# Softmax cross-entropy, one core: full loads alternate between the SyncE ring and the GpSimd ring

## The chip, the cores and the metric

The kernel runs on one core of a Trainium2 chip; the other cores are idle. The metric is the device time of one execution in microseconds, as a median of several runs on the same chip. The profile comes from one more look at such a run, taken by the hardware profiler; its span is some 1.8 us shorter than the time quoted. All runs of the two kernels compared here are in the fast state (granted clock 1.0).

## The reference

```python
def reference(logits, labels):            # logits 16 x 512 x 32000 float32, labels 16 x 512
    m = np.max(logits, axis=-1, keepdims=True)
    lse = np.log(np.sum(np.exp(logits - m), axis=-1)) + m.squeeze(-1)
    log_probs = logits - lse[..., None]
    return -log_probs[batch_index, seq_index, labels]
```

8192 rows of 32,000 logits are read once: 1048.6 MB. For each row the kernel needs the sum of exponentials (it leaves the maximum out) and one logit, the one that the label names.

## The kernel before

Each of the 128 partitions owns 64 rows (g = 0 to 63). A full load brings half a row per partition, 128 x 16,000 float32 (8.192 MB, printed by the profile as 8000.0 KB), into one of three buffers; ScalarE takes the exp in place and accumulates the sum. First and last rows are cut finer, so that the pipeline fills and drains quickly.

```python
W = 16000
data = ctx.enter_context(tc.tile_pool(name="data", bufs=3))
# ...
nc.gpsimd.iota(idx[:], pattern=[[V, G]], base=0, channel_multiplier=G * V)
nc.gpsimd.tensor_tensor(out=idx[:], in0=idx[:], in1=labs32, op=ALU.add)
for g in range(G):                         # 64 gathers of 128 single logits, all at the start
    nc.gpsimd.indirect_dma_start(
        out=lab_logit[:, g:g + 1], out_offset=None, in_=lg,
        in_offset=bass.IndirectOffsetOnAxis(ap=idx[:, g:g + 1], axis=1))
# ...
for j, (g, b, at, n) in enumerate(loads):  # 139 loads, 124 of them full
    if b not in buffers:
        buffers[b] = data.tile([P, W], FP32, tag="t", name="t")
    t = buffers[b]
    # ...
    nc.sync.dma_start(out=t[:, at:at + n], in_=lg_pg[:, g, c0:c0 + n])
    exp(g, t[:, at:at + n])                # ScalarE, in place, accum_out = the sum
    # ... log and subtraction for the rows near the end
```

A load waits for the exp that last used its buffer; the framework puts that wait on the issuing engine.

The softmax here doesn't subtract the row's maximum and nothing guards it: scores larger than these inputs give would overflow.

Of the kernel before, what the change touches and what calls it, by code (L numbers as in the profile page):

```python
# [1 line left out]

# [5 lines left out]

FP32 = mybir.dt.float32  # L10
I32 = mybir.dt.int32


EXP = mybir.ActivationFunctionType.Exp
LN = mybir.ActivationFunctionType.Ln
ALU = mybir.AluOpType
X = mybir.AxisListType.X


@with_exitstack  # L20
def kernel(
    ctx: ExitStack,
    tc: tile.TileContext,
    logits: bass.AP,
    labels: bass.AP,
    out: bass.AP,
):
    nc = tc.nc

    B, S, V = logits.shape  # L30
    P = 128
    G = B * S // P
    W = 16000


    lg = logits.rearrange("b s v -> (b s) v")
    lg_pg = lg.rearrange("(p g) v -> p g v", g=G)
    labels_pg = labels.rearrange("b s -> (b s)").rearrange("(p g) -> p g", g=G)
    out_pg = out.rearrange("b s -> (b s)").rearrange("(p g) -> p g", g=G)



    loads = []

    def plan(g, widths_by_buffer, order):

        n_buffers = 1 + max((l[1] for l in loads), default=-1)
        for b, i in order:
            ws = widths_by_buffer[b]
            loads.append((g, n_buffers + b, sum(ws[:i]), ws[i]))  # L50

    plan(0, [[4000, 4000, 8000], [16000]], [(0, 0), (0, 1), (0, 2), (1, 0)])
    for g in range(1, G - 2):
        plan(g, [[W], [W]], [(0, 0), (1, 0)])
    plan(G - 2, [[W], [10000, 6000]], [(0, 0), (1, 0), (1, 1)])
    plan(
        G - 1,
        [[7400, 5840, 2260], [4540, 3720, 2920, 1780, 1460, 1120], [960]],
        [(0, 0), (0, 1), (1, 0), (1, 1), (1, 2), (0, 2), (1, 3), (1, 4), (1, 5), (2, 0)],
    )  # L60
    assert sum(l[3] for l in loads) == G * V

    data = ctx.enter_context(tc.tile_pool(name="data", bufs=3))
    persist = ctx.enter_context(tc.tile_pool(name="persist", bufs=1))

    labs64 = persist.tile([P, G], mybir.dt.int64)
    labs32 = labs64[:].bitcast(I32).rearrange("p (g two) -> p g two", two=2)[:, :, 0]
    idx = persist.tile([P, G], I32)
    lab_logit = persist.tile([P, G], FP32)
    K = 10  # L70
    sums = persist.tile([P, G - 1, 5], FP32)
    sums_last = persist.tile([P, K], FP32)
    totals = persist.tile([P, G - 1], FP32)
    logsum = persist.tile([P, G - 1], FP32)
    res = persist.tile([P, G - 1], FP32)
    part = persist.tile([P, 1], FP32)
    logsum_last = persist.tile([P, 1], FP32)
    res_last = persist.tile([P, 1], FP32)

    ctx.enter_context(tc.manual_schedule())  # L80


    nc.scalar.dma_start(out=labs64[:], in_=labels_pg)
    nc.scalar.preload_act_table_set("natural_log_exp_and_others")  # L84
    nc.vector.memset(sums[:], 0.0)  # L85
    nc.gpsimd.iota(idx[:], pattern=[[V, G]], base=0, channel_multiplier=G * V)  # L86
    nc.gpsimd.tensor_tensor(out=idx[:], in0=idx[:], in1=labs32, op=ALU.add)  # L87
    for g in range(G):
        nc.gpsimd.indirect_dma_start(  # L89
            out=lab_logit[:, g:g + 1],  # L90
            out_offset=None,
            in_=lg,
            in_offset=bass.IndirectOffsetOnAxis(ap=idx[:, g:g + 1], axis=1),
        )


    buffers = {}
    col = {}
    n_exp = {}

    def exp(g, ap):
        k = n_exp.get(g, 0)
        n_exp[g] = k + 1
        s = sums[:, g, k:k + 1] if g < G - 1 else sums_last[:, k:k + 1]
        nc.scalar.activation(out=ap, in_=ap, func=EXP, accum_out=s)  # L105

    for j, (g, b, at, n) in enumerate(loads):
        if b not in buffers:
            buffers[b] = data.tile([P, W], FP32, tag="t", name="t")
        t = buffers[b]  # L110
        c0 = col.get(g, 0)
        col[g] = c0 + n
        nc.sync.dma_start(out=t[:, at:at + n], in_=lg_pg[:, g, c0:c0 + n])  # L113
        exp(g, t[:, at:at + n])

        left = len(loads) - 1 - j
        if left == 6:
            nc.vector.reduce_sum(out=totals[:], in_=sums[:], axis=X)  # L118
        if left == 4:
            nc.scalar.activation(out=logsum[:], in_=totals[:], func=LN)  # L120
            nc.vector.tensor_tensor(out=res[:], in0=logsum[:], in1=lab_logit[:, 0:G - 1], op=ALU.subtract)  # L121
        if left == 1:
            nc.vector.reduce_sum(out=part[:], in_=sums_last[:, 0:K - 1], axis=X)  # L123
    assert n_exp[G - 1] == K
    nc.sync.dma_start(out=out_pg[:, 0:G - 1], in_=res[:])

    nc.scalar.activation(out=logsum_last[:], in_=sums_last[:, K - 1:K], func=LN, bias=part[:])  # L127
    nc.vector.tensor_tensor(out=res_last[:], in0=logsum_last[:], in1=lab_logit[:, G - 1:G], op=ALU.subtract)  # L128
    nc.sync.dma_start(out=out_pg[:, G - 1:G], in_=res_last[:])


# [1 line left out]
_INS = ['logits', 'labels']  # L133
_OUTS = [((16, 512), 'float32')]


# [23 lines left out]
```

## Time and profile before

| | before |
|---|---|
| time, median of 3 runs | 2435.72 us |
| bytes read | 1048.67 MB, 431 GB/s over the span |
| DMA engines busy with logits | 99.8% |
| ScalarE busy | 72% |
| a full load, landing to landing | 18.90 us |
| an exp of one full load | 13.54 + 0.19 us |

The first fence is the profile's page of the kernel before. The rows with digits show the busy share, in tenths, of 40 equal slices of the span; the queue lines give packets, MB and the share of the 16 DMA engines' time; a group's line gives busy us, mean ns of one, then the engine's idle time before these instructions and what ended it.

```profile
span 2434.1 us, 807 instructions
...
DVE 1.3 (0%) x5; ACT 1748.9 (72%) x281; POOL 61.0 (3%) x70
...
DMA  9999999999999999999999999999999999999998
GB/s 421 422 421 433 425 438 431 427 438 438 433 426 436 438 434 426 435 438 434 426 435 436 435 430 431 436 435 430 431 436 438 431 427 436 438 433 426 438 433 377
...
q1 hardware_dynamic: 20304, 1048.62, 99.8%
q0 software_dynamic: 2048, 0.04, 0.1%
...
L105 ACT ACTIVATE t<-t 128x16000 f32<-128x16000 f32 (+5 forms) x139 | 1734.8, 12481 | 681.4 <-DMA t<-in_logits_dram 681.2
...
```

The DMA engines are full in every slice but the last and almost everything is on one queue, q1. ScalarE (ACT) idles 681 us, and what ends its idle time is a load. That makes the kernel DMA-bound. The wait on SyncE's queue looks large and is harmless:

```profile
...
SPq L113 <- ACT t L105: 2330.9, 125, 26.6
...
```

The columns are us in total, times and the longest wait. SyncE waits for free buffers because more than enough is queued already. In the timeline of the steady part (start us, us, what; in brackets the idle time before it) an exp starts every 18.9 us after 5.3 us of waiting:

```profile
...
386.87 13.54 ACT L105 ACTIVATE t<-t 128x16000 f32<-128x16000 f32 x1 [5.30 <-DMA t<-in_logits_dram]
...
405.78 13.54 ACT L105 ACTIVATE t<-t 128x16000 f32<-128x16000 f32 x1 [5.28 <-DMA t<-in_logits_dram]
...
```

And the windows view (us, then busy us and count of VectorE, ScalarE and GpSimd, granted clock, DMA share, GB/s; a share can print as 1.01, as neighbouring packet records overlap by some ns) separates the stretch with gathers from the one without:

```profile
...
61.50:301.00 239.50, 0.00 (x0) 172.21 (x25) 41.32 (x44) 1.00 1.01 427
301.00:2159.00 1858.00, 0.00 (x0) 1340.05 (x197) 0.00 (x0) 1.00 1.00 433
...
```

While gathers run, GB/s is 427 instead of 433. The trace also records every DMA packet. In the steady part one packet is one partition's row of a load, 64,000 bytes in 2361 to 2369 ns, and they stand end to end. Shorter rows at both ends of the kernel (4480 bytes in 173 ns, 32,000 in 1185 ns) put all sizes from 4480 bytes up within 2% of a line: 27.2 GB/s per engine, and 8 ns per packet. 16 engines at 27.2 GB/s are 435 GB/s, which is the ceiling that the Trainium skill derives ("DMA: Bandwidth & Descriptors", section "Where 436 GB/s comes from"). This trace agrees: the steady part is within 0.4% of it.

### The profile page before, as it was taken

What the parts mean: (1) busy time and instruction counts of PE and PEld (TensorE: products, weight loads), DVE (VectorE), ACT (ScalarE), POOL (GpSimd) and SP (SyncE); (2) the same over time, 40 slices, a digit from 0 to 9 for tenths busy, and PEclk for the clock granted to TensorE, in tenths of its full rate; (3) what the DMA queues carried; (4) which work ended last, traced back from release to release, by engine and by line L of the source; (5) the groups of instructions that cost most, each with busy time, mean ns of one, the idle gap of its engine ahead of it and who ended that gap; (6) DMA issues with size and microseconds to landing.
All of it is one profiled execution on the core that took longest, in us unless ns stands there. A gap on an engine that the chain in (4) does not pass through costs nothing.

```text
span 2434.1 us, 807 instructions
## 1 busy us (share of the span) xinstructions
DVE 1.3 (0%) x5; ACT 1748.9 (72%) x281; POOL 61.0 (3%) x70
## 2 busy tenths in 40 slices
DVE  0000000000000000000000000000000000000000
ACT  4777766777677776777677776777667776777769
POOL 3222000000000000000000000000000000000000
DMA  9999999999999999999999999999999999999998
GB/s 421 422 421 433 425 438 431 427 438 438 433 426 436 438 434 426 435 438 434 426 435 436 435 430 431 436 435 430 431 436 438 431 427 436 438 433 426 438 433 377
DMA packets 22502, 1048.77 MB, mean 431 GB/s; under 512 B 4576, under 2 KB 4704, under 8 KB 5216
## 3 DMA queue, kind: packets, MB, share of 16 engines
q1 hardware_dynamic: 20304, 1048.62, 99.8%
q0 software_dynamic: 2048, 0.04, 0.1%
q10 hardware_dynamic: 144, 0.07, 0.0%
q14 instruction: 6, 0.05, 0.0%
HBM read 1048.67 MB, written 0.03 MB: 431 GB/s over the span
## 4 chain that ended last, share of the span: by engine, by line
DMA 76%; ACT 24%; issue 0%; SPq 0%; ACTq 0%; DVE 0%
DMA t<-in_logits_dram 76%; ACT t L105 24%; SPq L113 0%; ACTq L105 0%; ACT logsum_last L127 0%; DVE res_last L128 0%; ACT logsum L120 0%
## 5 line engine op out<-in xcount | busy, mean ns | idle before, releaser
L105 ACT ACTIVATE t<-t 128x16000 f32<-128x16000 f32 (+5 forms) x139 | 1734.8, 12481 | 681.4 <-DMA t<-in_logits_dram 681.2
L89 POOL DMA_INDIRECT lab_logit<-in_logits_dram,idx x64 | 60.3, 942 | 178.3 <-DMA lab_logit<-in_logits_dram,idx 174.5
L105 ACT ACTIVATION_READ_ACCUMULATOR t<-t 128x1 f32 x139 | 25.9, 186 | 0.0
L84 ACT ACT_TABLE_LOAD x1 | 1.3, 1283 | 1.2 <-PEq L144 1.2
L118 DVE TENSOR_REDUCE totals<-sums 128x63 f32<-128x315 f32 x1 | 0.5, 480 | 2398.9 <-ACT t L105 2398.9
L87 POOL TENSOR_TENSOR idx<-idx,labs 128x64 int32<-128x64 int32 x1 | 0.3, 322 | 7.5 <-DMA labs<-in_labels_dram 7.5
L85 DVE MEMSET sums<- 128x315 f32 x1 | 0.3, 321 | 0.9 <-PEq L144 0.9
L127 ACT ACTIVATE logsum_last<-sums_last,part 128x1 f32<-128x1 f32 x1 | 0.3, 294 | 0.0
L121 DVE TENSOR_TENSOR res<-logsum,lab_logit 128x63 f32<-128x63 f32 x1 | 0.2, 225 | 25.3 <-ACT logsum L120 25.3
L120 ACT ACTIVATE logsum<-totals 128x63 f32<-128x63 f32 x1 | 0.2, 238 | 0.0
L86 POOL IOTA idx<- 128x64 int32 x1 | 0.2, 172 | 0.4 <-PEq L155 0.4
L123 DVE TENSOR_REDUCE part<-sums_last 128x1 f32<-128x9 f32 x1 | 0.2, 163 | 4.0 <-ACT t L105 4.0
L128 DVE TENSOR_TENSOR res_last<-logsum_last,lab_logit 128x1 f32<-128x1 f32 x1 | 0.2, 159 | 1.2 <-ACT logsum_last L127 1.2
L144 POOL MEMSET const-uint8-127<- 128x1 uint8 x1 | 0.1, 118 | 0.0
L144 POOL MEMSET const-bfloat16-1.0<- 128x1 bf16 x1 | 0.1, 113 | 0.0
L144 POOL MEMSET const-float32-0.0<- 128x1 f32 x1 | 0.1, 98 | 0.2 <-issue 0.2
L144 POOL MEMSET const-float32-1.0<- 128x1 f32 x1 | 0.1, 104 | 0.0
## 6 DMA issues: line engine op xcount, KB each, us to landing
t<-in_logits_dram SPq DMA_DIRECT2D x124, 8000.0 KB, 43.0
t<-in_logits_dram SPq DMA_DIRECT2D x1, 5000.0 KB, 35.9
t<-in_logits_dram SPq DMA_DIRECT2D x2, 2000.0 KB, 9.6
t<-in_logits_dram SPq DMA_DIRECT2D x1, 4000.0 KB, 21.4
t<-in_logits_dram SPq DMA_DIRECT2D x1, 3700.0 KB, 32.9
t<-in_logits_dram SPq DMA_DIRECT2D x1, 3000.0 KB, 42.6
t<-in_logits_dram SPq DMA_DIRECT2D x1, 2920.0 KB, 39.5
t<-in_logits_dram SPq DMA_DIRECT2D x1, 2270.0 KB, 26.4
```

Source lines behind the costliest of these rows:

```text
L84: nc.scalar.preload_act_table_set("natural_log_exp_and_others")
L85: nc.vector.memset(sums[:], 0.0)
L86: nc.gpsimd.iota(idx[:], pattern=[[V, G]], base=0, channel_multiplier=G * V)
L87: nc.gpsimd.tensor_tensor(out=idx[:], in0=idx[:], in1=labs32, op=ALU.add)
L89: nc.gpsimd.indirect_dma_start(out=lab_logit[:, g:g + 1], out_offset=None, in_=lg, in_offset=bass.IndirectOffsetOnAxis(ap=idx[:, g:g + 1], ...
L105: nc.scalar.activation(out=ap, in_=ap, func=EXP, accum_out=s)
L118: nc.vector.reduce_sum(out=totals[:], in_=sums[:], axis=X)
L120: nc.scalar.activation(out=logsum[:], in_=totals[:], func=LN)
L121: nc.vector.tensor_tensor(out=res[:], in0=logsum[:], in1=lab_logit[:, 0:G - 1], op=ALU.subtract)
L123: nc.vector.reduce_sum(out=part[:], in_=sums_last[:, 0:K - 1], axis=X)
L127: nc.scalar.activation(out=logsum_last[:], in_=sums_last[:, K - 1:K], func=LN, bias=part[:])
L144: nc = _bacc.Bacc("TRN2", target_bir_lowering=False, num_devices=1)
```

## The change

The intent is to use both DMA rings that the core has, SyncE's hardware ring and GpSimd's software ring, in turn for the full loads numbered 4 to 123, and to spread the 64 gathers: as GpSimd's queue is in order, gathers ahead of its loads would hold them up, so two stand behind each GpSimd load until all 64 are out. Loads are also written ahead of the exp that precedes them, so that GpSimd's program order is right; buffers, sizes and exps stay.

```diff
+    shared = range(4, 124)
+
+    def ring(j):
+        return nc.gpsimd if j in shared and j % 2 == 1 else nc.sync
 ...
-    for g in range(G):
+    def gather(g):
         nc.gpsimd.indirect_dma_start(
 ...
+    to_gather = list(range(G))
 ...
-    for j, (g, b, at, n) in enumerate(loads):
+    def load(j):
+        g, b, at, n = loads[j]
         if b not in buffers:
             buffers[b] = data.tile([P, W], FP32, tag="t", name="t")
-        t = buffers[b]
 ...
-        nc.sync.dma_start(out=t[:, at:at + n], in_=lg_pg[:, g, c0:c0 + n])
-        exp(g, t[:, at:at + n])
+        ring(j).dma_start(out=buffers[b][:, at:at + n], in_=lg_pg[:, g, c0:c0 + n])
+        if ring(j) is nc.gpsimd:
+            for _ in range(2):
+                if to_gather:
+                    gather(to_gather.pop(0))
+
+    loaded = 0
+    for j, (g, b, at, n) in enumerate(loads):
+        while loaded < len(loads) and loads[loaded][1] < b + 3:
+            load(loaded)
+            loaded += 1
+        exp(g, buffers[b][:, at:at + n])
```

More of the change, by code (lines that the diff above doesn't have):

```diff
@@ L123 @@
             nc.vector.reduce_sum(out=part[:], in_=sums_last[:, 0:K - 1], axis=X)
-    assert n_exp[G - 1] == K
+    assert n_exp[G - 1] == K and not to_gather
     nc.sync.dma_start(out=out_pg[:, 0:G - 1], in_=res[:])
```

## The prediction

> **What bounds the kernel now.** The 16 DMA engines. The page's DMA row is 9 in all slices but the last, queue 1 keeps them busy for 99.8% of the span, and 1048.67 MB come in at 431 GB/s. ScalarE is busy 72% and in the steady part waits 5.27 us for each load (timeline): loads land every 18.90 us (56.70 us per three in the chain of waits), an exp takes 13.54 + 0.19 us. SyncE waits only for buffers (2330.9 us in total, 125 times): with three buffers, work is always queued.
>
> In the trace's packet records the steady part (301 to 2159 us) has 64,000-byte packets, one row each, of 2361 to 2369 ns, back to back: 8 and a 9 ns semaphore packet are the 18.90 us. Shorter rows (4480 bytes: 173 ns; 32,000: 1185 ns) put a line through these of 27.2 GB/s per engine plus about 8 ns per packet. The Trainium skill ("DMA: Bandwidth & Descriptors", section "Where 436 GB/s comes from") gives a ceiling of 435.2 GB/s; this trace runs at 433 in the steady part. At most 0.4% is left there, whoever issues.
>
> Outside it: about 2 us of start, about 6 us of gathers (early on three loads take 57.9 instead of 56.7 us), and a short tail.
>
> **What the change does.** 60 of the 124 full loads move to GpSimd's ring; buffers, bytes, exps and tail stay. The gathers spread from 247 us to some 1200 us.
>
> - Bandwidth: both rings feed the same 16 engines. The skill (same page, "Issuing engines are not separate DMA queues") says they interleave there and only issue time is saved; no run yet shows it for large loads. Issue time is hidden already. Gain 0.
> - Switching rings: in the gather period a 64,000-byte packet after a gather's 9 ns semaphore packet still takes 2361 to 2369 ns, so a switch costs nothing visible. Cost 0.
> - Gathers: each adds 24 ns of own packets per engine and makes the next large packet about 65 ns longer; 64 of them are about 6 us in either kernel. Change 0.
> - Software packets: a gather's 8 elements went as one 32-byte packet, so software packets can hold several descriptors. If a whole load's share (8 rows) went as one, 7 x 8 ns are saved per load, 60 loads: -3.5 us (estimate). If rows were cut into 4 KB packets, 15 x 8 ns per row would be added: about +58 us, 2.4%. I hold rows kept whole for much likelier.
> - Order: two loads now share the engines, so landings become uneven (about 16.5 and 21.3 us, or in pairs), but with three buffers one load's data is always queued when another is finished. No idle engine. GpSimd's issue is hidden behind queued work.
>
> **Predicted time:** 2433 us, 8 in 10 between 2427 and 2446. Faster by over 2%: 0.02; within 2%: 0.93; slower by over 2%: 0.05.
>
> **What would show it.** Right: DMA row still 9, two queues at about 50% each, sum of two landing intervals 37.8 us, ScalarE still 72% busy. Wrong: software packets under 64,000 bytes, DMA slices below 9, or steady GB/s off 433.
>
> **What would make it wrong.** Software packets cut small; descriptor fetch for the software ring slowing large packets; one engine lagging so that landings come late; a tail that starts out of phase; or gathers costing more beside software loads.

## The result

| | before | after |
|---|---|---|
| time, median of 4 runs each | 2435.72 us | 2436.28 us (2436.11 to 2436.45) |
| ratio of the fast runs | | 1.0002, 95% interval 0.9985 to 1.002 |
| GB/s over the span | 431 | 431 |
| ScalarE busy | 1748.9 us | 1746.8 us |

A ratio is the mean time of one kernel's fast runs over that of the other's of the same rounds, so it is not quite the ratio of the medians quoted.

The profile's page of the kernel after, the same parts as above and the group of GpSimd's loads:

```profile
span 2434.7 us, 804 instructions
...
DVE 1.3 (0%) x5; ACT 1746.8 (72%) x281; POOL 95.2 (4%) x130
...
DMA  9999999999999999999999999999999999999998
GB/s 422 437 424 434 437 422 437 436 425 434 435 425 435 435 423 437 435 423 437 435 423 436 437 434 426 436 436 435 428 433 436 436 429 430 437 437 432 426 436 374
...
q1 hardware_dynamic: 11664, 557.09, 53.1%
q0 software_dynamic: 10688, 491.56, 46.8%
...
L111 ACT ACTIVATE t<-t 128x16000 f32<-128x16000 f32 (+5 forms) x139 | 1734.4, 12478 | 683.4 <-DMA t<-in_logits_dram 683.3
L119 POOL DMA_DIRECT2D t<-in_logits_dram x60 | 33.3, 555 | 2160.0 <-ACT t L111 2120.1
...
```

The traffic is now split 53 to 47 over two queues, q1 (SyncE) and q0 (GpSimd), and little else on the page has moved: the DMA row is full, ScalarE's busy and idle times are those of before within 0.3%, and GpSimd is busy 95 us instead of 61. q0's packets add up as 60 loads x 128 rows = 7680, 60 x 16 semaphore packets = 960, and 2048 of the gathers (as before): 10,688. So the software ring sends whole rows of 64,000 bytes too; it neither cuts nor joins them. GpSimd's 60 issues cost it 0.56 us each.

The windows of the kernel after:

```profile
...
61.50:301.00 239.50, 0.00 (x0) 174.36 (x27) 14.91 (x18) 1.00 1.00 432
301.00:2159.00 1858.00, 0.00 (x0) 1327.22 (x197) 74.81 (x99) 1.00 1.00 433
...
```

The gathers' loss has moved, from the first 300 us (where it was 427 GB/s, now 432) into the long stretch, where it is too thin to show in these lines (from 300 to 1300 us it is 432 GB/s after and 434 before). In the packet records of one DMA engine (records do not name the engine; packets are strung together by each one's start meeting the end of the one before) the two rings take turns row by row:

```
start us   ns    bytes  queue
1602.337  2361   64000  q0
1604.695  2364   64000  q1
1607.055  2366   64000  q0
1609.417  2369   64000  q1
1616.504     9       4  q0     semaphore packet at the end of a load
1616.510  2366   64000  q1
```

(Two packets left out after the fourth. The starts are in the trace's own time, 10.46 us ahead of the time from the span's start in which the views count.) A change of ring costs nothing that these records show. The turn-taking agrees with the Trainium skill, "DMA: Bandwidth & Descriptors", section "Queues, rings and completion order": each engine goes round its rings packet by packet.

What did change is the rhythm. Timeline of the kernel after, while gathers stand behind the GpSimd loads:

```profile
...
1004.63 13.54 ACT L111 ACTIVATE t<-t 128x16000 f32<-128x16000 f32 x1 [17.08 <-DMA t<-in_logits_dram]
...
1018.17 13.52 ACT L111 ACTIVATE t<-t 128x16000 f32<-128x16000 f32 x1
...
1035.51 13.54 ACT L111 ACTIVATE t<-t 128x16000 f32<-128x16000 f32 x1 [3.73 <-DMA t<-in_logits_dram]
...
1049.83 13.54 ACT L111 ACTIVATE t<-t 128x16000 f32<-128x16000 f32 x1 [0.69 <-DMA t<-in_logits_dram]
...
1080.55 13.54 ACT L111 ACTIVATE t<-t 128x16000 f32<-128x16000 f32 x1 [17.09 <-DMA t<-in_logits_dram]
```

Exps start 13.5, 17.3, 14.3 and 30.7 us apart, in a repeating pattern of four loads in some 76 us, so the mean is still 18.9 us. It goes on until about 1440 us, some 200 us after the last gather; from then on they are 18.9 us apart, but for a few. ScalarE once waits 17 us for a load and once finds the next one there already. The DMA engines never run out meanwhile: in the packet records from 300 to 2200 us there is no moment with fewer than half of the engines active.

### The profile page after: what moved, and what is told of

Its sections match the earlier page's. It is cut to its first block, busy times and chain, and to the rows that moved or that the text cites. A ratio compares the mean times of both kernels' runs of the same rounds, so it can differ in the third digit from the quotient of the medians.

```text
span 2434.7 us, 804 instructions
## 1 busy us (share of the span) xinstructions
DVE 1.3 (0%) x5; ACT 1746.8 (72%) x281; POOL 95.2 (4%) x130
## 4 chain that ended last, share of the span: by engine, by line
issue 49%; DMA 36%; ACT 13%; another core or an unknown queue 1%; POOL 1%; SPq 0%; POOLq 0%; ACTq 0%; DVE 0%
DMA t<-in_logits_dram 36%; ACT t L111 13%; POOL t L119 1%; SPq L119 0%; POOL lab_logit L94 0%; POOLq L119 0%; ACT logsum_last L144 0%; ACTq L111 0%; DVE res_last L145 0%; ACT logsum L137 0%; POOLq L172 0%
## 5 line engine op out<-in xcount | busy, mean ns | idle before, releaser
L119 POOL DMA_DIRECT2D t<-in_logits_dram x60 | 33.3, 555 | 2160.0 <-ACT t L111 2120.1
L111 ACT ACTIVATION_READ_ACCUMULATOR t<-t 128x1 f32 x139 | 25.9, 186 | 0.0
```

The source lines that it names most:

```text
L111: nc.scalar.activation(out=ap, in_=ap, func=EXP, accum_out=s)
L119: ring(j).dma_start(out=buffers[b][:, at:at + n], in_=lg_pg[:, g, c0:c0 + n])
```

## Experiments

The theory to test: the time is the packet time of 16 engines, which ring sends a load does not matter to them, the gathers cost the same in both kernels, and the order of landings is absorbed by the buffers. The rivals: two effects cancel (a gain of two rings against a loss at the gathers, or the other way about), or the software ring has a cost that the hardware ring covers.

### Without gathers, both kernels

```diff
-    for g in range(G):
-        nc.gpsimd.indirect_dma_start( ... )
+    nc.gpsimd.memset(lab_logit[:], 0.0)        # kernel before; wrong result on purpose
```
```diff
-    to_gather = list(range(G))
+    to_gather = []                             # kernel after; wrong result on purpose
+    nc.gpsimd.memset(lab_logit[:], 0.0)
```

> The kernel before without its 64 gathers (wrong result on purpose: lab_logit is 0). Theory (time is the 16 engines' packet time, gathers cost the same in either kernel): about 6 us less than before, 2429.5 us (2428.5 to 2431), because each gather costs an engine 24 ns of its own packets and some 65 ns in the packet behind it. Rival (the spread gathers hide a gain or a loss of the second ring): nothing different is expected of this run alone, it must be read with after_no_gather.

> The changed kernel without gathers (wrong result on purpose), so loads on two rings alone. Theory: within 1 us of before_no_gather, about 2430 us, with both at about 433.7 GB/s in the steady part. Rival A (two rings carry more and the spread gathers take it back): 3 us or more below before_no_gather. Rival B (two rings cost something and spread gathers cost less): 3 us or more above it.

Measured: 2430.77 us (2430.72 to 2431.03) and 2431.16 us (2431.13 to 2431.45), beside 2435.72 us of the kernel before on the same chip. Both results are wrong, as intended. The gathers are worth 4.95 us before (2435.72 - 2430.77) and 5.12 us after (2436.28 - 2431.16, medians). The two rings alone differ by 0.4 us. So there is no pair of effects that cancel: loads on two rings gain nothing and lose next to nothing, and spreading the gathers neither saves nor costs.

Page of the kernel after without gathers, queue lines:

```profile
span 2429.4 us, 732 instructions
...
q1 hardware_dynamic: 11664, 557.09, 53.1%
q0 software_dynamic: 8640, 491.52, 46.8%
...
```

8640 = 7680 rows + 960 semaphore packets, with 2429.4 us of span beside 2434.7. In this kernel exps start 18.9 us apart from the tenth full load on; the pattern of 13.5 to 30.7 us is gone. So that pattern comes with the gathers behind the loads, not with the two rings as such. Why the gathers lock the loads into it I have not tried to settle; it costs no time here.

### All gathers ahead of the GpSimd loads

```diff
-    to_gather = list(range(G))
+    to_gather = []
+    for g in range(G):
+        gather(g)
```

> The changed kernel with all 64 gathers ahead of GpSimd's first load, as the kernel before has them. Theory: the engines' packet work is unchanged, but GpSimd's queue is in order and its first load (the sixth load of all) is issued only after the last gather; the trace of before shows the last gather at 247 us under full traffic, less when the engines run dry. The engines then idle some 50 to 110 us: 2490 to 2550 us, and afterwards the same pace. Rival (where the gathers stand does not matter, as gathers are cheap): 2436 us.

Measured: 2485.0 us (2484.95 to 2485.2), ratio 1.0202, correct. The direction is the theory's, the size is just under the range I gave. Windows and timeline of this kernel:

```profile
...
60.00:140.00 80.00, 0.00 (x0) 13.63 (x2) 42.67 (x46) 1.00 0.38 153
...
```

```profile
...
129.41 0.94 POOL L94 DMA_INDIRECT lab_logit<-in_logits_dram,idx  x1 [0.30 <-issue]
130.35 1.16 POOL L121 DMA_DIRECT2D t<-in_logits_dram  x2
152.26 13.54 ACT L113 ACTIVATE t<-t 128x16000 f32<-128x16000 f32 x1 [77.09 <-DMA t<-in_logits_dram]
...
```

From 60 to 140 us the engines are 38% busy, which is 0.62 x 80 = 49.6 us idle, and the kernel is 49.3 us slower. GpSimd's first load goes out at 130.35 us, behind the last gather, and ScalarE has waited 77 us for it. My range was too high because I took the gathers' slow pace under traffic (4.8 us each) too far: once the engines ran dry they went out every 1.25 us. Putting the gathers behind the loads is therefore a necessary part of this change, not an ornament.

### All full loads on GpSimd

```diff
-        return nc.gpsimd if j in shared and j % 2 == 1 else nc.sync
+        return nc.gpsimd if j in shared else nc.sync
```

> All 120 full loads from the fifth on through GpSimd's software ring, two gathers behind each of the first 32. Theory: the ring does not matter, rows stay whole packets of 64,000 bytes and GpSimd's issue is hidden behind a queued load: 2436 us (2434 to 2440), evenly spaced landings of 18.9 us as in before. Rival B (software-ring loads are slower by some per cent, and in the changed kernel the hardware ring filled their gaps): 2445 us or more.

Measured: 2445.60 us (2445.46 to 2445.7), ratio 1.004, correct. My expectation missed: this is the rival's number. But the windows show no slow ring in the steady part:

```profile
...
75.00:100.00 25.00, 0.00 (x0) 25.00 (x5) 4.66 (x6) 1.00 0.73 302
...
1300.00:2300.00 1000.00, 0.00 (x0) 722.32 (x106) 27.44 (x52) 1.00 1.00 434
...
```

434 GB/s from 1300 to 2300 us, as before; the loss is at the ends. From 75 to 100 us the engines are 73% busy (some 7 us lost): load 4, issued by GpSimd at 9 us, takes turns with SyncE's loads 2 and 3, which were issued earlier and are needed earlier (one engine's packet records alternate between the two rings from 13.5 to 40.6 us), so that load 2 lands at 41 us instead of 23 and its buffer comes free that much later. At the other end SyncE's last loads overtake the GpSimd loads before them (the records alternate again, from 2304 to 2339 us), and the timeline shows ScalarE waiting 24 us and then working through what has piled up, without a pause:

```profile
...
2306.41 13.54 ACT L111 ACTIVATE t<-t 128x16000 f32<-128x16000 f32 x1 [7.63 <-DMA t<-in_logits_dram]
...
2344.21 13.54 ACT L111 ACTIVATE t<-t 128x16000 f32<-128x16000 f32 x1 [24.17 <-DMA t<-in_logits_dram]
...
2357.75 13.52 ACT L111 ACTIVATE t<-t 128x16000 f32<-128x16000 f32 x1
...
```

That reading, hand-over between rings instead of a slow software ring, is a new theory, and needed its own run.

### Every load on GpSimd, from the first

```diff
-        return nc.gpsimd if j in shared and j % 2 == 1 else nc.sync
+        return nc.gpsimd
 ...        # iota and add for the gathers' indices are moved behind the first five loads;
 ...        # two gathers still follow each load from the fifth on
```

> All 139 loads of logits on GpSimd's software ring, the index arithmetic moved behind the first four loads. after_all_gpsimd took 2445.6 us instead of 2436; its trace shows 434 GB/s from 1300 to 2300 us as before, but 394 GB/s in the first 100 us, where a GpSimd load overtakes an earlier SyncE load, and ScalarE idle for 24 us at 2320 us, where SyncE loads overtake the last GpSimd loads. Theory (the loss is the change of ring at both ends, not the software ring): with one ring throughout it is gone, 2436 us (2434.5 to 2439), landings 18.9 us apart. Rival (software loads are slow to start or need more queued work): 2443 us or more again.

Measured: 2436.94 us (2436.91 to 2437.19), beside 2435.94 us of the kernel before: ratio 1.0004. The 10 us are gone; how they divide between the two ends was not measured. One ring throughout, of either kind, is the same speed within 0.04%:

```profile
span 2435.4 us, 803 instructions
...
q0 software_dynamic: 22000, 1048.62, 99.8%
...
```

### Two hardware rings

```diff
-        return nc.gpsimd if j in shared and j % 2 == 1 else nc.sync
+        return nc.scalar if j in shared and j % 2 == 1 else nc.sync
-        if ring(j) is nc.gpsimd:
+        if ring(j) is nc.scalar:
```

(The gathers stay on GpSimd and run ahead, as in the kernel before.)

> Three buffers, SyncE's and ScalarE's hardware rings alternating on the same 120 loads. Theory: as after, 2436 us (2434.5 to 2439), since the engines are the limit and three buffers hide uneven landings. Rival (the software ring held back a gain that two hardware rings have): under 2425 us.

Measured: 2435.72 us (2435.51 to 2435.88) beside 2435.85 us, ratio 0.9999. No gain that the software ring was holding back.

### Two buffers instead of three

If the third buffer is what absorbs the order of landings, then taking it away should hurt two rings and not one. Four kernels, the same two edits each (in the kernel before, the first alone), on top of the kernel before, after, gpsimd_from_first and sync_scalar:

```diff
-    data = ctx.enter_context(tc.tile_pool(name="data", bufs=3))
+    data = ctx.enter_context(tc.tile_pool(name="data", bufs=2))
-        while loaded < len(loads) and loads[loaded][1] < b + 3:     # not in the kernel before
+        while loaded < len(loads) and loads[loaded][1] < b + 2:
```

> The kernel before with two buffers of 64,000 bytes per partition in place of three. Theory: loads land 18.9 us apart, a buffer is free 13.7 us after its landing, so the next load is queued 5.2 us before the engines run out: 2436 us (2435 to 2441).

> The changed kernel with two buffers. Theory (alternating rings make landings uneven and the third buffer is what hides it): the two loads in flight share the engines, their landings come closer than the 13.7 us that a buffer's exp takes, and the engines run out now and then: 2445 to 2500 us, DMA slices at 8 or 9 and less GB/s, clearly above before_2buf. Rival (one ring or two makes no difference to how much must be queued): within 3 us of before_2buf.

> All loads on the software ring, as in gpsimd_from_first, with two buffers. after_2buf lost 65 to 112 us where before_2buf lost nothing. Theory (two unordered rings make landings uneven): one ring, here the software one, lands loads 18.9 us apart again, so 2437 us (2435.5 to 2441). Rival (what two buffers can't hide is the software ring's longer way from a freed buffer to the first packet): 2455 us or more.

> Two buffers, and the 60 loads that after gives to GpSimd on ScalarE's hardware ring instead (gathers run ahead on GpSimd as in before). Theory (two rings, whatever their kind): landings uneven, the engines dry at times, 2450 to 2560 us as after_2buf. Rival (the software ring): 2436 to 2441 us.

> after_2buf once more, as its profile fell in the run of 2548 us and its runs scatter (2500 to 2548 us) where every other kernel's agree within 1 us. Expected: scatter again, no run under 2490 us, as small differences at the start decide how close two landings come; a profile in which ScalarE's exp ends less than 1 us before the next landing, so that the next load is queued when nothing is left.

| two buffers | time, median of all runs (lowest to highest) | ratio to before, fast runs |
|---|---|---|
| one ring, SyncE (before_2buf) | 2436.22 (2435.93 to 2436.26) | 1.0001 |
| one ring, GpSimd (gpsimd_from_first_2buf) | 2437.77 (2437.74 to 2438.48) | 1.0009 |
| two rings, SyncE and GpSimd (after_2buf) | 2515.47 (2500.44 to 2548.17) | 1.0306 |
| the same again | 2512.97 (2494.03 to 2544.37) | 1.0291 |
| two rings, SyncE and ScalarE (sync_scalar_2buf) | 2543.53 (2542.71 to 2549.0) | 1.0447 |

All are correct. It is two rings that need the third buffer, whatever their kind: one ring loses under 2 us (medians), two rings lose 58 us at least. after_2buf lies above the range that I gave (2445 to 2500 us). The runs of after_2buf scatter by 2%; by the rule used here (over 1.5% above the fastest of the same kernel) its slowest runs count as slow, both its profiles fell into such a run, and its clock is 1.0 all the same. Why they scatter stays open. The lines below are therefore from sync_scalar_2buf, whose runs agree.

Windows of the kernel before with two buffers, and of the two rings with two buffers:

```profile
...
1300.00:2300.00 1000.00, 0.00 (x0) 719.99 (x107) 0.00 (x0) 1.00 1.00 433
...
```

```profile
...
1300.00:2300.00 1000.00, 0.00 (x0) 687.81 (x101) 0.00 (x0) 1.00 0.97 412
...
```

The DMA share falls from 1.00 to 0.97 and GB/s from 433 to 412; in the packet records from 1300 to 2200 us no packet at all is under way for 2.1% of the time, where the kernel before with two buffers has no such moment. In the timeline of that kernel each load lands alone, 18.9 us after the one before:

```profile
...
1408.51 13.54 ACT L105 ACTIVATE t<-t 128x16000 f32<-128x16000 f32 x1 [5.27 <-DMA t<-in_logits_dram]
...
1427.41 13.54 ACT L105 ACTIVATE t<-t 128x16000 f32<-128x16000 f32 x1 [5.27 <-DMA t<-in_logits_dram]
...
```

The timeline of the two rings with two buffers shows how the engines run dry:

```profile
...
1402.29 0.33 ACTq L119 DMA_DIRECT2D t<-in_logits_dram  x1
1414.10 13.54 ACT L111 ACTIVATE t<-t 128x16000 f32<-128x16000 f32 x1 [11.85 <-DMA t<-in_logits_dram]
...
1427.76 40.35 SPq L119 DMA_DIRECT2D t<-in_logits_dram  x2
1428.26 13.54 ACT L111 ACTIVATE t<-t 128x16000 f32<-128x16000 f32 x1 [0.53 <-DMA t<-in_logits_dram]
...
1454.12 13.54 ACT L111 ACTIVATE t<-t 128x16000 f32<-128x16000 f32 x1 [12.23 <-DMA t<-in_logits_dram]
...
```

At 1427.76 an exp has ended and SyncE's load is issued into the freed buffer. At 1428.26, 0.5 us later, the load issued at 1402.29 has landed and its exp starts. From then on the only queued load is half a microsecond old and has yet to begin, so the engines run dry. The next load lands at about 1454.1, 25.9 us later. A pair of loads takes 39.6 to 40.0 us (1388.63, 1428.26, 1468.30) instead of 37.8.

The packet records show how the sharing brings two landings so close. On one engine (times as in the timeline; the others are alike) the older load, SyncE's, has the engine to itself for seven of its eight rows, from 1389.1 us on. Then the younger load's first row starts at 1406.40, the older's last row at 1408.76, the younger's second at 1411.11, and the older's semaphore packet at 1413.47. So the older load lands two packets later than it would have alone, and only six rows of the younger are left. They end at 1427.6, 14.2 us later, just after the exp of the older (13.7 us) has freed its buffer. The next load's first row starts at 1428.7 at the earliest, and on most engines this first row after the pause takes 2.5 to 3.3 us instead of 2.36. With one ring, as the lines of the kernel before with two buffers show, the next load is issued 5.3 us before a landing, and its rows wait behind it.

### Rows cut into 4000-byte pieces

The prediction's main fear was small software packets. This kernel cuts the rows of the 120 shared loads by reading every other 4000 bytes (the sum of exps over both halves is the same, so the result stays correct):

```diff
+        src, dst = lg_pg[:, g, c0:c0 + n], buffers[b][:, at:at + n]
+        if n == W and j in range(4, 124):
+            src = lg_pg[:, g, :].rearrange("p (a two c) -> p a two c", two=2, c=1000)[:, :, c0 // W, :]
+            dst = dst.rearrange("p (a c) -> p a c", c=1000)
-        ring(j).dma_start(out=buffers[b][:, at:at + n], in_=lg_pg[:, g, c0:c0 + n])
+        ring(j).dma_start(out=dst, in_=src)
```

> The changed kernel with each of the 120 shared loads cut into rows of 16 pieces of 1000 elements (every other 4000 bytes of the logits' row; the same sums, correct result). Tests what I feared of software packets, and the 8 ns per packet. Theory: 16 packets of 147 + 8 ns in place of one of 2365 ns, 0.95 us more per load, 114 us more for 120 loads: 2550 us (2530 to 2570) if both rings send each piece as a packet of its own; about 2493 us if the software ring joins pieces into larger packets (as it joined a gather's 8 elements) and only the hardware ring pays. Rival (small packets cost nothing here as the engines hide it): 2436 us.

Measured: 2572.61 us (2572.52 to 2573.57), ratio 1.0562. The page's traffic row and queue lines:

```profile
...
GB/s 407 410 411 410 410 412 410 411 410 410 412 411 411 410 410 412 410 411 411 410 411 412 412 413 412 413 412 412 413 412 412 412 412 412 412 412 412 420 313 373
...
q1 hardware_dynamic: 126864, 557.09, 53.8%
q0 software_dynamic: 64448, 491.56, 46.8%
...
```

q1 has 122,880 packets of 4000 bytes (60 loads x 128 x 16), q0 has 61,440 of 8000: the software ring does join pieces, in pairs. It gains it little, as the packet records have 312.9 ns for a joined packet and 159.8 for a single one, so a join saves at most 7 ns of 320. (The records overlap by some ns; from start to start, in 1500 to 1560 us, it is 309 and 156 ns, and a join saves about 2.) The steady part runs at 412 GB/s; 8.192 MB at that rate are 19.88 us per load, 0.98 us more than 18.90, 118 us for 120 loads. I had put 0.95 us on it. That number was near, but my expectation as a whole missed: the total is 2.6 us above the range that I gave for pieces sent one by one, and where the software ring joins pieces, as it did, I had expected 2493 us. From start to start a piece of 4000 bytes costs about 8 ns over its 147 ns, alone or joined. Whether reading every other 4000 bytes of memory adds to this was not tried apart. The rest, 137 - 118 = 19 us, is at the end (313 GB/s in the last slice but one): ScalarE waits 36.8 us there for the last GpSimd load, which took 63 us from issue to landing (2407.5 to 2471.0), beside SyncE loads of whole 64,000-byte rows. That is the hand-over of rings again, and sharper: from 2425 to 2465 us the packet records have 256 packets of 8000 bytes from q0 and 239 rows of 64,000 from q1. The engines take turns by packet, whatever its size, so the GpSimd load got about an eighth of the bytes. Small pieces do cost, then, and the changed kernel escapes that cost as its software packets are whole rows.

## Why the prediction was right

The prediction was 2433 us (2427 to 2446), the same within 2%; measured 2436.28. Point by point:

- *"The 16 DMA engines" bound the kernel.* Right. Four kernels with three buffers and different rings (SyncE, SyncE and GpSimd, GpSimd alone, SyncE and ScalarE) lie between 2435.7 and 2436.9 us; a fifth (after_all_gpsimd, 2445.6) loses its 10 us at the ends, not in the steady part. The runs do not separate what sets a packet's 2361 ns, the engines themselves or the memory and the ways behind them; the answer to the change does not depend on it.
- *"Bandwidth: ... Gain 0."* Right: 0.4 us between the two kernels without gathers. The skill's statement (same page, section "Issuing engines are not separate DMA queues") holds for loads of 8 MB in these runs.
- *"Switching rings: ... Cost 0."* Right: 2361 to 2369 ns rows one after another from q0 and q1.
- *"Gathers: ... about 6 us in either kernel. Change 0."* The change is right; the size is 5.0 (before) and 5.1 us (after).
- *"If a whole load's share (8 rows) went as one ... -3.5 us (estimate)."* This term was wrong. The software ring sends each 64,000-byte row as its own packet. Taking it out of the sum moves 2433 to 2436.5, which is the measured time, as all other terms were 0. I drew it from a gather's eight 4-byte elements in one packet; of the pieces of 4000 bytes the ring joined only two at a time, and a join saved about 2 ns, not 8. The stated range held the result with this term or without it.
- *"If rows were cut into 4 KB packets ... about +58 us."* It did not happen; forced on 120 loads it cost 118 us in the steady part, 59 us per 60 loads, though on the software ring the pieces went in pairs, which the estimate did not foresee.
- *"Order: ... (about 16.5 and 21.3 us, or in pairs)."* Pairs came nearest: exps start 13.5, 17.3, 14.3 and 30.7 us apart while gathers stand behind the loads, and an even 18.9 us later on and without gathers. The sign that I named, two intervals that sum to 37.8 us, failed in the first of these (30.9, then 45.0; four sum to some 76). What I concluded from it, no idle engine with three buffers, was right, and the two-buffer kernels show that it was the buffers that made it so.

## What to carry to other kernels

Where the DMA engines' packets stood end to end, a second ring added no bandwidth; look at the packet time, not at the waits of the issuing queues. A second ring does change the order: loads issued later on another ring share the engines with earlier ones, which needs a spare buffer (with three it was free, with two it cost 58 us and more) and care at both ends, where loads change from one ring to another (10 us in after_all_gpsimd, nothing in the changed kernel). If one ring is enough, the kernel before shows that it needs only two of its three buffers: 2436.2 us with 64,000 bytes less per partition.

No run here beats the kernel before. The only time left that the runs show is the gathers' 5 us; a way to pick the label's logit without small DMA reads was not tried.

## What the Trainium skill lacked or had wrong

- "DMA: Bandwidth & Descriptors", section "Issuing engines are not separate DMA queues": it says that several issuing engines only save issue time. For bandwidth the runs agree (2435.7 to 2436.9 us over four choices of ring), but it doesn't say that it can cost: with two buffers, two rings took 2513 to 2544 us where one took 2436 to 2438 us (medians), because a later load takes every other packet from an earlier one.
- The same page, section "SWDGE vs HWDGE vs iDMA", has packets of at most 4096 bytes "preferably". The software ring's packets in these traces had 64,000 bytes (7680 of them in the changed kernel), and 8000 bytes where rows were cut into 4000-byte pieces; an engine gave one such packet to a ring before the other's turn.
- The same page, section "Why small descriptors are slow (HBM only)", holds packetizing worthwhile only at 256 bytes and below. It is not contradicted: a join of two 4000-byte pieces saved at most 7 ns of 320. In these runs 8 ns per packet and 27.2 GB/s per engine fit all rows from 4480 to 64,000 bytes within 2%, and 4000-byte pieces still cost 5% of the bandwidth (412 instead of 433 GB/s).
- No page tells what a small gather costs beside bulk loads: 24 ns of its own packets per engine, and about 60 ns more for the next large packet (about 2425 instead of 2365 ns), together 5 us for 64 gathers of 128 elements.
